# Layer 1's first feed-forward product as pinned 2x2 block products, and layer 2's modulation rows dealt out over output phases, chain and residual

## The chip, the cores and the metric

The kernel runs on one core of one Trainium2 chip. A core has a matrix engine (TensorE, PE in the profile), a vector engine (DVE), an activation engine (ACT), a general engine (POOL) and a sequencer that issues the transfers (SP). Each takes its own instructions in order. The metric is the device time of one execution in microseconds (us), lower is better.

## The reference, cut to what matters

A backbone of two trunk layers over 640 tokens (128 of context, 512 latent), model width 1024, feed-forward width 2816. Context tokens and latent tokens have different conditioning vectors, so each modulation value exists twice.

```
mod = jax.nn.silu(cond) @ p['w_mod'][l] + p['b_mod'][l]        # 6 * 1024 values, for each of 2 conditions
sh_a, sc_a, g_a, sh_f, sc_f, g_f = jnp.split(mod[:, None, :], 6, axis=-1)
xn = rmsnorm(h, p['norm_mix'][l]) * (1 + sc_a) + sh_a
...                                                            # three mixer branches, among them the delta-rule chain
h = h + g_a * y
xf = rmsnorm(h, p['norm_ffn'][l]) * (1 + sc_f) + sh_f
gu = xf @ p['ffn_w_in'][l]                                     # the first feed-forward product
h = h + g_f * ((jax.nn.silu(gu[..., :D_FF]) * gu[..., D_FF:]) @ p['ffn_w_out'][l])
```

## The kernel before, in words

Activations lie with features on the 128 partitions and 640 tokens on the free axis, in two halves of 320 (c = 0, 1). The code counts layers from 0: layer 1 of this text has l = 0, layer 2 has l = 1.

**Products.** A weight block of four 128x128 tiles comes by a transfer of 256 KB (tile wr). ACT rounds it (wh, L514), and POOL (L518) or DVE (L516) takes the remainder (wl). Each 128x128 by 128x320 product is made of three matmuls, high by high, low by high and high by low (lines L563, and L555 for block products). One "128x320" matmul is the unit of work on PE.

**Feed-forward.** The width of 2816 is 22 tiles f. For each f there are a gate product fg and an up product fu (8 k-tiles x 3 x 2 halves = 48 matmuls each, 96 for the pair). The output product is accumulated in groups of f: after each group, fo{group}_{d} for d = 0 to 7 multiplies the group's tiles into the eight output tiles, and the post-processing (h_update, L756, three DVE instructions) adds it to the residual h. Layer 1 has the two groups (0..10), (11..21), all plain. Layer 2 has three groups (0..7), (8..14), (15..21): its first 3 f are plain, and each of the other 19 pairs is made as a 2x2 block product with 7 instead of 8 block multiplications (class Pair; 7 x 4 x 3 = 84 matmuls instead of 96). The price is sums of weight blocks on DVE (L543), sums of token blocks ahead of it (token_sums), and sums of results. In the block stage strict[0] is set: ACT and DVE instructions that go through o() are held in the order in which the program wrote them on their engine.

**Modulation rows.** Class ModVe makes rows m of 48 (6 parts x 8 tiles). For each row a transfer brings the weights (tile wmt, half a row, 256 KB, when nh = 2; a whole row, 512 KB, when nh = 1), and for each of the two conditions one DVE reduction (L638, followed by a read of its accumulator) multiplies it with the conditioning vector and sums up. cond(h) loads half h of the two conditioning vectors (tile cbb) and applies silu: for each condition a tanh on ACT (L624) and one DVE instruction (L625). The wmt tile has bufs slots; a transfer into a slot waits on SP until the reductions that read it are done. In layer 1 the rows 16 to 35 (nh = 2, bufs 4: 80 reductions) run in the delta-rule chain, rows 36 to 39 in the layer's residual product (wo0 to wo7), rows 40 to 47 and all 48 rows of layer 2 in the posts of layer 1's fu products (nh = 1, bufs 4). Layer 2 itself makes no rows.

**Residual and join.** wo0 to wo7 is the mixer's output projection. The posts of its products update h, square it (ACT), and add the square (nacc, DVE L687). wo7 is done in two halves of tokens; each half's end starts the norm (ACT L691, a PE sum cs, ACT L575 and L577), the scaled activations (us L727 or L708, then xh on ACT and xl on DVE, L732 to L734, in layer 1 of before L713 and L720), and these feed the first feed-forward product. This stretch is called the join.

Where an instruction stands on its engine is set by a scheduler over program order and priorities; transfers are all issued by SP, in order.

Of the kernel before, what the change touches and what calls it, by code (L numbers as in the profile page):

```python
# [18 lines left out]
P = 128  # L19
# [11 lines left out]
GROUPS = (((0, 11), (11, 22)), ((0, 8), (8, 15), (15, 22)))  # L31
NPL = (22, 3)
# [380 lines left out]
def tile_hybrid(ctx: ExitStack, tc, a):  # L413
# [197 lines left out]
    class ModVe:  # L611
# [15 lines left out]
        def steps(self, l, ms):  # L627
# [3 lines left out]
            for h in range(self.nh):  # L631
                if self.nh > 1:
                    self.cond(h)
                for m in ms:
                    wm = self.pool.tile([P, self.w], F32, name="wmt", tag="wmt", bufs=self.bufs)
                    dma(wm, a["wmodt"][l, m][:, h * self.w:(h + 1) * self.w])
                    for i in range(2):
                        ins = ve.tensor_tensor_reduce(self.t, wm, self.c[:, i], 0.5, 0.0, ALU.mult, ALU.add,  # L638
                                                      accum_out=acc[h][:, m - m0, i:i + 1])
                        if OPT["pin"] in (1, 2 + self.nh):  # L640
                            tc.keep_in_program_order(ins)
# [8 lines left out]
    def mod_fix(mod, prm, s, d0=0, n=8):  # L650
# [7 lines left out]
        elif s == 2 or s == 5 and mod is mods[0]:  # L658
            ve.tensor_scalar(mod[:, sl], mod[:, sl], 0.5, None, op0=ALU.mult)
# [899 lines left out]
    class Blocks:  # L1559
# [26 lines left out]
        def snap(self, q, i):  # L1586
            t = self.s[q.name, i] = self.sn.tile([P, HF], F32, name="sn", tag="sn", bufs=4)
            o(se.activation(t, self.ps(q, 0), AF.Copy))
# [50 lines left out]
    for l in range(L):  # L1639
# [39 lines left out]
        gr, npl = GROUPS[l], NPL[l]  # L1679
# [127 lines left out]
    for l in range(L):  # L1807
# [107 lines left out]
        with pool("gt", "right", 2) as gt:  # L1915
# [11 lines left out]
            with pool("zs", "left") as zs:  # L1927
# [6 lines left out]
                with pool("bd", "left") as bd, pool("kp", "left") as kp:  # L1934
# [5 lines left out]
                    mst = ModVe(bd, 4, 2).steps(0, range(16, 16 + OPT["mc"])) if l == 0 else iter(())  # L1940
# [14 lines left out]
                    if l == 0:  # L1955
                        mod_fix(mod, prm, 2)
# [15 lines left out]
        mv = ModVe(mvp, 4, 1) if l + 1 < L else None  # L1972
        nm = Norm()
        resid_posts([f"wo{d}.{l}" for d in range(8)], hs, mod[:, 16:24], nm)
        for d in range(7):
            G.to(f"wo{d}.{l}")
            if l == 0:
                mv.run(0, range(16 + OPT["mc"] + (24 - OPT["mc"]) * min(d, 5) // 5, 16 + OPT["mc"] + (24 - OPT["mc"]) * min(d + 1, 5) // 5))
        if l == 0:
            mod_fix(mod, prm, 3)  # L1980
            mod_fix(mod, prm, 4)
        mark(f"normf{l}")
        gr, npl = GROUPS[l], NPL[l]
# [13 lines left out]
        with ExitStack() as fctx:  # L1997
# [8 lines left out]
            def g_post(f):  # L2006
                def post(ps):
                    th = tmp()
                    if l == 0:
                        se.activation(v3(th), ps, AF.Tanh, scale=0.5)  # L2010
                        ve.scalar_tensor_tensor(v3(th), v3(th), 1.0, ps, op0=ALU.add, op1=ALU.mult)
                    else:
                        se.activation(v3(th), ps, AF.Silu)
# [3 lines left out]
            def u_post(f, j):  # L2017
                def post(ps):
# [3 lines left out]
                    if l + 1 < L:  # L2022
                        if l == 0 and f < 8:
                            mv.run(0, [40 + f])
                            if f == 7:
                                mod_fix(mod, prm, 5)
                        mv.run(l + 1, range(48 * f // NF, 48 * (f + 1) // NF))
                return post

            gl_ = len(gr) - 1  # L2030
            for gi, (f0, f1) in enumerate(gr):
# [3 lines left out]
                if gi < gl_:  # L2035
                    for d in range(8):
                        G.posts[f"fo{gi}_{d}.{l}"] = lambda ps, d=d: h_update(hs, d, ps, mod[:, 40:48])
# [64 lines left out]
```

## Time and profile before

| what | value |
|---|---|
| median of three timed executions | 2867.09 us (2866.7 to 2870.57) |
| profiled execution, own time | 2866.79 us |
| its span, first to last instruction | 2865.0 us |
| mean granted TensorE clock | 0.968 of full speed |
| PE busy | 2681.8 us, 94% |
| DVE / ACT / POOL busy | 59% / 45% / 38% |

PE is the engine that is nearly always busy. The times of stretches are read from windows of this one profiled execution; it lies 0.3 us under the median of the timed ones.

### The profile page before, as it was taken

To read this page: it belongs to the slowest core of one execution; us is meant where nothing else is said; L and a number is where in the kernel's file an instruction comes from. 1 tells how busy PE (TensorE), PEld (TensorE's weight loads), DVE (VectorE), ACT (ScalarE), POOL (GpSimd) and SP (SyncE) were. 2 spreads that over 40 slices of the span, in tenths; PEclk is the share of its full clock that TensorE was granted. 3 is DMA by queue.
4 is the path that set the end of the run, shared out by engine and by line. 5 is a ranking of instruction groups with operands and counts; after the bars stand their busy time and mean duration, and the time that the engine had idled before them with its cause. 6 is when DMAs were issued, how large, how long until landed. Compare 5 with 4: busy or idle time off the path is not lost. (4 is left out here: it accounts for less than half of the span.)

```text
span 2865.0 us, 49715 instructions
## 1 busy us (share of the span) xinstructions
PE 2681.8 (94%) x19216; PEld 2461.6 (86%) x19216; DVE 1699.1 (59%) x3141; ACT 1290.1 (45%) x2431; POOL 1075.7 (38%) x777
## 2 busy tenths in 40 slices
PE   6889999899999999999998899997999998999998
PEld 4788887787878899999988888886877898999997
DVE  4765684647655699268456666757434345637373
ACT  5665655543333522122356646565333336425254
POOL 3543222343425467456544432333433254120203
PEclk9999999999999999999999999998999999999999
DMA  6254433245542355335323444232433331222222
GB/s 207 90 163 142 94 77 100 81 113 175 151 113 86 133 175 181 107 123 159 114 80 106 152 136 95 73 97 76 118 98 84 84 108 52 85 85 78 78 80 79
DMA packets 291836, 317.10 MB, mean 111 GB/s; under 512 B 163696, under 2 KB 174768, under 8 KB 291472
## 3 DMA queue, kind: packets, MB, share of 16 engines
q1 hardware_dynamic: 291600, 313.92, 37.4%
q8 instruction: 152, 2.49, 0.4%
q14 instruction: 84, 0.69, 0.1%
HBM read 266.01 MB, written 47.82 MB: 110 GB/s over the span
## 5 line engine op out<-in xcount | busy, mean ns | idle before, releaser
L518 POOL TENSOR_TENSOR wl<-wr,wh 128x512 fp32r<-128x512 f32 (+1 forms) x500 | 723.3, 1450 | 1407.0 <-ACT wh L514 1287.0
L563 PE MATMUL gm<-xh,wh 128*128 128x320 f32 x2848 | 706.2, 324 | 25.6 <-ACT xh L713 7.0
L563 PE MATMUL gm<-xl,wh 128*128 128x320 f32 x2848 | 692.0, 318 | 10.1 <-DVE xl L720 4.2
L563 PE MATMUL gm<-xh,wl 128*128 128x320 f32 x2848 | 687.3, 317 | 15.0 <-POOL wl L518 15.0
L514 ACT ACTIVATE wh<-wr 128x512 fp32r<-128x512 f32 (+1 forms) x538 | 332.4, 621 | 703.7 <-PE gm L563 441.6
L563 PEld LDWEIGHTS gm<-xh,wh 128*128 128x128 f32 x2848 | 487.3, 193 | 50.9 <-ACT xh L713 9.9
L563 PEld LDWEIGHTS gm<-xl,wh 128*128 128x128 f32 x2848 | 491.8, 192 | 27.0 <-DVE xl L720 9.0
L563 PEld LDWEIGHTS gm<-xh,wl 128*128 128x128 f32 x2848 | 489.5, 192 | 23.9 <-POOL wl L518 17.5
L638 DVE CUSTOM_DVE_ANT_0 ctb<-wmt,cbb 128x1024 f32<-128x1024 f32 (+1 forms) x200 | 298.2, 1491 | 3.4
L756 DVE SCALAR_TENSOR_TENSOR h<-gm,mod,h 128x128 f32<-128x128 f32 x168 | 63.8, 433 | 248.7 <-PE gm L563 248.6
L563 PE MATMUL gm<-ah,wh 128*128 128x320 f32 x704 | 164.2, 310 | 0.4 <-DVE h L756 0.2
L563 PE MATMUL gm<-ah,wl 128*128 128x320 f32 x704 | 163.3, 309 | 0.5 <-POOL wl L518 0.5
L563 PE MATMUL gm<-al,wh 128*128 128x320 f32 x704 | 163.3, 309 | 0.0
L1081 ACT ACTIVATE VN<-ch 64x64 f32<-64x64 f32 x320 | 69.9, 219 | 179.7 <-DVE vs L1078 165.5
L563 PEld LDWEIGHTS gm<-ah,wh 128*128 128x128 f32 x704 | 118.3, 188 | 1.7 <-DVE h L756 1.4
L563 PEld LDWEIGHTS gm<-ah,wl 128*128 128x128 f32 x704 | 118.4, 188 | 0.8 <-POOL wl L518 0.8
L563 PEld LDWEIGHTS gm<-al,wh 128*128 128x128 f32 x704 | 118.5, 188 | 0.2
L563 PE MATMUL gm<-ol,wh 128*128 128x320 f32 x384 | 99.0, 331 | 1.5 <-POOL ol L568 1.5
L563 PE MATMUL gm<-oh,wh 128*128 128x320 f32 x384 | 98.4, 333 | 0.5 <-DVE gth L1756 0.3
L563 PE MATMUL gm<-oh,wl 128*128 128x320 f32 x384 | 96.1, 326 | 0.0
L555 PE MATMUL gm<-xh,wl 128*128 128x320 f32 x304 | 94.0, 309 | 0.0
L555 PE MATMUL gm<-xl,wh 128*128 128x320 f32 x304 | 93.9, 309 | 0.0
(793 smaller groups left out, 4743.8 us busy)
## 6 DMA issues: line engine op xcount, KB each, us to landing
wr<-in_wall_dram SPq DMA_DIRECT2D x394, 256.0 KB, 3.0
wmt<-in_wmodt_dram SPq DMA_DIRECT2D x60, 512.0 KB, 3.7
wr<-in_wfo_dram SPq DMA_DIRECT2D x64, 256.0 KB, 2.7
wr<-in_wbr_dram SPq DMA_DIRECT2D x48, 256.0 KB, 2.7
wmt<-in_wmodt_dram SPq DMA_DIRECT2D x40, 256.0 KB, 3.4
wq<-in_wall_dram SPq DMA_DIRECT2D x38, 256.0 KB, 3.1
wm<-in_wmod_dram SPq DMA_DIRECT2D x16, 512.0 KB, 8.4
wr<-in_wfo_dram SPq DMA_DIRECT2D x32, 192.0 KB, 2.4
```

The lines of the kernel that those rows point to most:

```text
L514: o(se.activation(wh[:, :w], wr[:, :w], AF.Copy))
L518: ge.tensor_tensor(wl[:, :w], wr[:, :w], wh[:, :w], op=ALU.subtract)
L555: o(pe.matmul(ps, w_[:, wsl], x_[k], start=(start and i == 0), stop=(stop and i == 2), skip_group_check=True))
L563: o(pe.matmul(ps[:, c, :HF], w_[:, wsl], x_[kx][:, c * HF:(c + 1) * HF], start=(start and i == 0), stop=(stop and i == 2)))
L638: ins = ve.tensor_tensor_reduce(self.t, wm, self.c[:, i], 0.5, 0.0, ALU.mult, ALU.add, accum_out=acc[h][:, m - m0, i:i + 1])
L756: o(ve.scalar_tensor_tensor(hs[d][:, s:e], ps[:, c, s - c * HF:e - c * HF], g[:, d, i:i + 1], hs[d][:, s:e], op0=ALU.mult, op1=ALU.add))
L1081: se.activation(VN[d * 64:(d + 1) * 64, h, n], ps[h * 64:(h + 1) * 64, 1], AF.Copy)
```

## The change

Both layers now use the groups (0..7), (8..14), (15..21) and 3 plain tiles, so layer 1's other 19 pairs become block products too, in the pinned order, with silu by ACT's Silu. The ModVe in the "mv" pool gets nh = 2 and bufs = 2 in place of nh = 1 and bufs = 4, so each set of rows loads the conditioning twice. The rows are dealt out anew: layer 1's rows 36 to 39 (mv0) and the first steps of 40 to 47 (mv1) in its residual product, the rest of mv1 behind its fu1 and fu2; layer 2's rows 0 to 23 (nxt) in the posts of layer 1's output products, 5 reductions for each d in group 0 and 4 in the later ones; its rows 24 to 39 in layer 2's own chain, and 40 to 47 in layer 2's residual product. Inside the pinned stage the reductions are pinned too.

```diff
-GROUPS = (((0, 11), (11, 22)), ((0, 8), (8, 15), (15, 22)))
-NPL = (22, 3)
+GROUPS = ((0, 8), (8, 15), (15, 22))
+NPL = 3
...
-                        if OPT["pin"] in (1, 2 + self.nh):
+                        if strict[0] or OPT["pin"] in (1, 2 + self.nh):
                             tc.keep_in_program_order(ins)
...
-            t = self.s[q.name, i] = self.sn.tile([P, HF], F32, name="sn", tag="sn", bufs=4)
+            t = self.s[q.name, i] = self.sn.tile([P, HF], F32, name="sn", tag="sn", bufs=3)
...
-                    mst = ModVe(bd, 4, 2).steps(0, range(16, 16 + OPT["mc"])) if l == 0 else iter(())
+                    mst = ModVe(bd, 4, 2).steps(l, range(16, 16 + OPT["mc"]) if l == 0 else range(24, 40))
...
-        mv = ModVe(mvp, 4, 1) if l + 1 < L else None
+        mv = ModVe(mvp, 2, 2)
+
+        def some(gen, n):
+            for _ in range(n):
+                if next(gen, 0) == 0:
+                    break
+
+        mv0 = mv.steps(l, range(16 + OPT["mc"], 40)) if l == 0 else iter(())
+        mv1 = mv.steps(l, range(40, 48))
+        nxt = mv.steps(l + 1, range(24)) if l + 1 < L else iter(())
         nm = Norm()
         resid_posts([f"wo{d}.{l}" for d in range(8)], hs, mod[:, 16:24], nm)
         for d in range(7):
             G.to(f"wo{d}.{l}")
-            if l == 0:
-                mv.run(0, range(16 + OPT["mc"] + (24 - OPT["mc"]) * min(d, 5) // 5, 16 + OPT["mc"] + (24 - OPT["mc"]) * min(d + 1, 5) // 5))
+            if l == 0 and d < 4:
+                some(mv0, 4)
+            else:
+                some(mv1, 5)
+        some(mv0, 1000)
...
+        else:
+            some(mv1, 1000)
+            mod_fix(mod, prm, 5)
...
-                    if l == 0:
-                        se.activation(v3(th), ps, AF.Tanh, scale=0.5)
-                        ve.scalar_tensor_tensor(v3(th), v3(th), 1.0, ps, op0=ALU.add, op1=ALU.mult)
-                    else:
-                        se.activation(v3(th), ps, AF.Silu)
+                    se.activation(v3(th), ps, AF.Silu)
...
-                    if l + 1 < L:
-                        if l == 0 and f < 8:
-                            mv.run(0, [40 + f])
-                            if f == 7:
-                                mod_fix(mod, prm, 5)
-                        mv.run(l + 1, range(48 * f // NF, 48 * (f + 1) // NF))
+                    if l == 0 and f:
+                        some(mv1, 8 if f < npl - 1 else 1000)
+                        if f == npl - 1:
+                            mod_fix(mod, prm, 5)
...
+            def fo_post(gi, d):
+                def post(ps):
+                    h_update(hs, d, ps, mod[:, 40:48])
+                    some(nxt, 4 if gi else 5)
+                return post
...
-                        G.posts[f"fo{gi}_{d}.{l}"] = lambda ps, d=d: h_update(hs, d, ps, mod[:, 40:48])
+                        G.posts[f"fo{gi}_{d}.{l}"] = fo_post(gi, d)
...
+            for d in range(6):
+                n = f"fo{gl_}_{d}.{l}"
+
+                def after(*args, post=G.posts[n]):
+                    post(*args)
+                    some(nxt, 4)
+                G.posts[n] = after
```

The order of instructions shows it at three places.

DVE, where layer 1 goes from group 0's output products into the block products of the next group. h_9516 is the last output tile (d = 7), ctb is the reductions' scrap, mod_103 layer 2's modulation. Before, the kernel has such an edge in layer 2 alone:

```order
L756 SCALAR_TENSOR_TENSOR h_23747<-gm,mod_103,h_23747 128x128
L756 SCALAR_TENSOR_TENSOR h_23747<-gm,mod_103,h_23747 128x192
L756 SCALAR_TENSOR_TENSOR h_23747<-gm,mod_103,h_23747 128x320
L516 TENSOR_TENSOR wl<-ws,wh 128x512 x2
L543 TENSOR_TENSOR ws<-wq 128x512
```

After the change, layer 1's edge reads:

```order
L756 SCALAR_TENSOR_TENSOR h_9516<-gm,mod_102,h_9516 128x320
L638 ISA ctb,mod_103<-wmt,cbb 128x512
L638 ISA mod_103 128x1
L638 ISA ctb,mod_103<-wmt,cbb 128x512
L638 ISA mod_103 128x1
L638 ISA ctb,mod_103<-wmt,cbb 128x512
L638 ISA mod_103 128x1
L638 ISA ctb,mod_103<-wmt,cbb 128x512
L638 ISA mod_103 128x1
L638 ISA ctb,mod_103<-wmt,cbb 128x512
L638 ISA mod_103 128x1
L516 TENSOR_TENSOR wl<-ws,wh 128x512 x2
```

Five reductions now stand between the last update and the two remainders wl of the next weights. At the edge from group 1 to group 2 there are four.

DVE, at the end of layer 1's residual product (h_9515 is d = 6, h_9516 is d = 7). Before:

```order
L687 TENSOR_TENSOR nacc<-nacc,th 128x640
L756 SCALAR_TENSOR_TENSOR h_9516<-gm,mod_102,h_9516 128x128
L756 SCALAR_TENSOR_TENSOR h_9516<-gm,mod_102,h_9516 128x192
L756 SCALAR_TENSOR_TENSOR h_9516<-gm,mod_102,h_9516 128x320
L708 TENSOR_TENSOR th<-us_10025,nacc 128x320
```

After:

```order
L687 TENSOR_TENSOR nacc<-nacc,th 128x640
L638 ISA ctb,mod_102<-wmt,cbb 128x512
L638 ISA mod_102 128x1
L756 SCALAR_TENSOR_TENSOR h_9516<-gm,mod_102,h_9516 128x128
L638 ISA ctb,mod_102<-wmt,cbb 128x512
L638 ISA mod_102 128x1
L756 SCALAR_TENSOR_TENSOR h_9516<-gm,mod_102,h_9516 128x192
L638 ISA ctb,mod_102<-wmt,cbb 128x512
L638 ISA mod_102 128x1
L638 ISA ctb,mod_102<-wmt,cbb 128x512
L638 ISA mod_102 128x1
L756 SCALAR_TENSOR_TENSOR h_9516<-gm,mod_102,h_9516 128x320
```

Between the conditioning's two L625 behind d = 4 and this last update stand 16 reductions. In layer 2's residual product, which had none, 16 stand ahead of d = 3's update, then the conditioning, and 16 more ahead of d = 6's.

ACT, in layer 1's second group of output products, where the second half of nxt's conditioning comes in; each pair of wh (128x512 and 128x384) is the weight of one d. Before, this place held only such weights:

```order
L514 ACTIVATE wh<-wr 128x512 x2
L514 ACTIVATE wh<-wr 128x384
L514 ACTIVATE wh<-wr 128x512 x2
```

After:

```order
L514 ACTIVATE wh<-wr 128x384
L514 ACTIVATE wh<-wr 128x512
L624 ACTIVATE ctb<-cbb 128x512 x2
L514 ACTIVATE wh<-wr 128x384
L514 ACTIVATE wh<-wr 128x512
```

Two tanh of the conditioning now stand ahead of the weight of d = 3's second half.

## Rows read from the trace of the kernel before

**Rows 1.** The page: busiest engine; two costliest weight preparations (busy, mean ns).

```profile
PE 2681.8 (94%) x19216; PEld 2461.6 (86%) x19216; DVE 1699.1 (59%) x3141; ACT 1290.1 (45%) x2431; POOL 1075.7 (38%) x777
...
L518 POOL TENSOR_TENSOR wl<-wr,wh 128x512 fp32r<-128x512 f32 (+1 forms) x500 | 723.3, 1450 | 1407.0 <-ACT wh L514 1287.0
...
L514 ACT ACTIVATE wh<-wr 128x512 fp32r<-128x512 f32 (+1 forms) x538 | 332.4, 621 | 703.7 <-PE gm L563 441.6
```

**Rows 2.** What PE waited for, 1000 to 1460 us, layer 1's feed-forward.

```profile
PE gm L563 <- POOL wl L518: 0.6, 1, 0.6
```

**Rows 3.** Windows: us, PE, PEld, DVE, ACT, POOL busy (count), PEclk, DMA share, GB/s.

```profile
1050.00:1100.00 50.00, 50.00 (x343) 50.00 (x342) 49.15 (x55) 11.33 (x19) 33.81 (x18) 1.00 0.57 181
2450.00:2500.00 50.00, 50.00 (x343) 50.00 (x342) 35.11 (x57) 24.73 (x44) 3.07 (x3) 1.00 0.25 79
```

**Rows 4.** Groups of DVE by form: busy us, mean ns, idle before.

```profile
L638 DVE CUSTOM_DVE_ANT_0 ctb<-wmt,cbb 128x512 f32<-128x512 f32 x80 | 68.7, 859 | 0.3
...
L638 DVE DVE_READ_ACCUMULATOR2_ANT mod<- 128x1 f32 x160 | 12.4, 78 | 0.0
```

**Rows 5.** Transfers: count, KB each, median us from issue to landing.

```profile
wmt<-in_wmodt_dram SPq DMA_DIRECT2D x40, 256.0 KB, 3.4
...
cbb<-in_condb_dram SPq DMA_DIRECT2D x2, 512.0 KB, 5.0
```

**Rows 6.** Line L638: shortest/median/longest ns, first and last start.

```profile
L638 DVE CUSTOM_DVE_ANT_0 ctb<-wmt,cbb x200: 673/1224/2480, 652.1 to 1390.3; 128x1024 f32<-128x1024 f32 x60, 128x512 f32<-128x512 f32 x40
```

**Rows 7.** Line L624, the conditioning's tanh on ACT, likewise.

```profile
L624 ACT ACTIVATE ctb<-cbb x6: 629/632/1064, 647.2 to 926.6; 128x512 f32<-128x512 f32 x4, 128x1024 f32<-128x1024 f32 x2
```

**Rows 8.** Line L625, the conditioning's DVE instruction, likewise.

```profile
L625 DVE SCALAR_TENSOR_TENSOR cbb<-ctb,cbb x6: 681/694/1227, 649.7 to 927.7; 128x512 f32<-128x512 f32 x4, 128x1024 f32<-128x1024 f32 x2
```

**Rows 9.** Timeline (start, us) of layer 2's edge from group 0 to block products.

```profile
2580.34 1.13 DVE L756 SCALAR_TENSOR_TENSOR h<-gm,mod,h 128x128 f32<-128x128 f32 x3 [5.31 <-PE gm L563]
...
2581.39 1.28 DVE L516 TENSOR_TENSOR wl<-ws,wh 128x512 fp32r<-128x512 f32 x2
...
2582.04 0.31 PE L555 MATMUL gm<-xl,wh 128*128 128x320 f32 x1
...
2582.19 0.35 PE L555 MATMUL gm<-xh,wl 128*128 128x320 f32 x1
```

**Rows 10.** Windows at and behind a PE stall of 4.83 us, in layer 2's first part.

```profile
1545.50:1551.00 5.50, 0.67 (x5) 0.41 (x3) 5.45 (x5) 1.78 (x4) 5.50 (x5) 0.74 0.30 116
1551.00:1555.00 4.00, 4.00 (x15) 4.00 (x16) 3.60 (x3) 0.30 (x1) 2.79 (x2) 0.51 0.68 211
```

**Rows 11.** Windows of 80 us around the joins of layers 1 and 2, alike in phase.

```profile
946.96:1026.96 80.00, 73.69 (x449) 69.30 (x448) 55.64 (x89) 39.79 (x74) 38.42 (x27) 0.94 0.34 110
2369.16:2449.16 80.00, 71.08 (x425) 66.46 (x424) 44.43 (x81) 47.96 (x86) 35.45 (x25) 0.91 0.19 59
```

**Rows 12.** Timeline of DVE at the end of layer 1's residual product.

```profile
954.26 1.13 DVE L756 SCALAR_TENSOR_TENSOR h<-gm,mod,h 128x128 f32<-128x128 f32 x3 [0.66 <-PE gm L563]
...
956.20 0.83 DVE L687 TENSOR_TENSOR nacc<-nacc,th 128x640 f32<-128x640 f32 x1 [0.81 <-ACT th L686]
...
976.96 0.55 DVE L756 SCALAR_TENSOR_TENSOR h<-gm,mod,h 128x320 f32<-128x320 f32 x1 [4.42 <-PE gm L563]
```

**Rows 13.** The same for layer 2's residual product.

```profile
2369.43 1.14 DVE L756 SCALAR_TENSOR_TENSOR h<-gm,mod,h 128x128 f32<-128x128 f32 x3 [4.27 <-PE gm L563]
...
2390.55 1.13 DVE L756 SCALAR_TENSOR_TENSOR h<-gm,mod,h 128x128 f32<-128x128 f32 x3 [4.28 <-PE gm L563]
...
2394.07 0.68 DVE L756 SCALAR_TENSOR_TENSOR h<-gm,mod,h 128x128 f32<-128x128 f32 x2 [0.75 <-PE gm L563]
2399.16 0.55 DVE L756 SCALAR_TENSOR_TENSOR h<-gm,mod,h 128x320 f32<-128x320 f32 x1 [4.42 <-PE gm L563]
```

**Rows 14.** Windows over the chains of layers 1 and 2, to the same place.

```profile
641.00:917.50 276.50, 269.48 (x2238) 222.24 (x2237) 174.91 (x490) 95.42 (x252) 103.59 (x78) 0.98 0.44 127
2071.00:2341.07 270.07, 263.80 (x2238) 219.41 (x2237) 109.86 (x322) 93.48 (x249) 99.78 (x79) 0.99 0.32 86
```

More of the change, by code (lines that the diff above doesn't have):

```diff
@@ L657, in mod_fix @@
                                     op0=ALU.add, op1=ALU.mult)
-        elif s == 2 or s == 5 and mod is mods[0]:
+        elif s == 2:
             ve.tensor_scalar(mod[:, sl], mod[:, sl], 0.5, None, op0=ALU.mult)
@@ L1678, in tile_hybrid @@
             k8(f"wo{d}", "post" if d == 7 else None)
-        gr, npl = GROUPS[l], NPL[l]
+        gr, npl = GROUPS, NPL
         pairs = {f: Pair(f"ff{f}.{l}", a["wall"][l, TILES[f"fg{f}"]], a["wall"][l, TILES[f"fu{f}"]]) for f in range(npl, NF)}
@@ L1954, in tile_hybrid @@
                         pass
-                    if l == 0:
-                        mod_fix(mod, prm, 2)
+                    for s_ in (2,) if l == 0 else (3, 4):
+                        mod_fix(mod, prm, s_)
                     G.to(f"br1_7.{l}")
@@ L1981, in tile_hybrid @@
             mod_fix(mod, prm, 4)
+        else:
+            some(mv1, 1000)
+            mod_fix(mod, prm, 5)
         mark(f"normf{l}")
-        gr, npl = GROUPS[l], NPL[l]
+        gr, npl = GROUPS, NPL
         if npl < NF:
@@ L2008, in post @@
                     th = tmp()
-                    if l == 0:
-                        se.activation(v3(th), ps, AF.Tanh, scale=0.5)
-                        ve.scalar_tensor_tensor(v3(th), v3(th), 1.0, ps, op0=ALU.add, op1=ALU.mult)
-                    else:
-                        se.activation(v3(th), ps, AF.Silu)
+                    se.activation(v3(th), ps, AF.Silu)
                     st[f] = th
@@ L2049, in tile_hybrid @@
             if l + 1 < L:
-                for s_ in range(6):
+                some(nxt, 1000)
+                for s_ in range(3):
                     mod_fix(mods[l + 1], prms[l + 1], s_)
```

## The prediction

> **What bounds the kernel now.** The page first: PE is busy 94% of the span, the next engine DVE 59% [rows 1]. A share is a mean over stages, so next the waits of PE in the stretch that the change rewrites, layer 1's feed-forward from 1000 to 1460 us: all there is comes to 0.6 us [rows 2]. Then windows inside it: 343 matmuls in 50 us with PE busy for all 50, at full clock, though DVE is busy for 49.15 of them with modulation rows [rows 3]. Layer 2's block stage, at 2450 us, runs at the same 343 in 50 us with DVE at 35.11 [rows 3]. So both kinds of feed-forward are bound by the number of matmuls, 50 / 343 = 0.1458 us each, and DVE's load there costs nothing today. What is gained is matmuls; what can be lost is a place where PE must wait for the work that is dealt out anew. One quantity decides most of these: the modulation rows take DVE time and a transfer each, and they move from where DVE's queue was harmless (behind plain products) to where PE waits for the very next DVE instruction.
>
> **Matmuls saved.** 19 pairs x 12 = 228 matmuls of 128x320 go, nothing is added on PE but what follows. 228 x 0.1458 = **-33.2 us**. Both rates of [rows 3] are equal, so this term holds as long as PE is fed.
>
> **The edges from output products to block products.** Layer 2 has this edge in before: the last update of h runs from 2580.34 for 1.13 us, right behind it the two remainders wl from 2581.39 for 1.28 us, so the first is ready about 2582.03, and PE uses it at 2582.19 [rows 9]. The slack is 0.16 us. In layer 1 after the change, five reductions (then four, at the second edge) stand in that gap, in pinned order. A reduction of 512 takes 0.859 us on average and the read of its accumulator 0.078 [rows 4], 0.94 together; the shortest of any is 0.673 [rows 6]. Five and four of them less the slack: 5 x 0.94 - 0.16 = 4.5 and 4 x 0.94 - 0.16 = 3.6, **+8.1 us**. From below, at 0.75 each: 3.6 + 2.8 = 6.4. From above: five steps are two and a half weight tiles, and there are two slots now, so the third tile may have to land (3.4 us [rows 5]) behind the first one's reductions, up to 3 us more: 11.1. The other six posts of a group hide theirs, since their h is not the last and the next product's weights are POOL's work.
>
> The Trainium skill, page "GPSIMD Engine Reference", section "Specifications", says that GpSimd shares its SBUF interfaces with VectorE and contends with DVE instructions that have two SBUF inputs, as a reduction has. Around an edge POOL is nearly idle (3.07 of 50 us in [rows 3]), so by that rule the edge's reductions would be short ones, and the term 6.4 instead of 8.1, the whole sum 1.7 lower. I keep the mean, since the rows don't tell short from long by what POOL did.
>
> **The conditioning's second half in group 1.** nxt has 24 rows x 2 = 48 reductions per half: 40 in group 0's eight posts, 8 in the posts of d = 0 and 1 of group 1. The next half of the conditioning goes into the same tile, so its transfer waits for reduction 48. A product of group 1 is 7 x 3 x 2 = 42 matmuls, 6.1 us. d = 1 ends 12.3 us into the group; h 1.13 and four reductions 3.75 make 17.1; the transfer lands 5.0 later [rows 5], 22.1; tanh 0.63 [rows 7], the DVE instruction 0.69 [rows 8], tanh again, 24.1. Only then does ACT do the weight of d = 3's second half, 0.62, and POOL its remainder, 1.45 [rows 1]: 26.1. PE is there at three products and four tiles, 18.4 + 3.5 = 21.9 us. So up to 4.0 us of PE; none if reduction 48 was early or the weight stands ahead in time. I take **+3.5** (0 to 4).
>
> **The clock behind these stalls.** Where PE is busy for only 0.67 of 5.50 us, a stall of 4.83, the clock falls: the window 1551 to 1555 behind it has PE busy for 4.00 us, a granted clock of 0.51, the lower of the two levels (1.2 GHz), and only 15 matmuls, where 27.4 would go at 343 in 50 us [rows 10]. The 12.4 that are missing are 1.8 us. My three stalls (4.5, 3.5, 3.6) are shorter than the 4.83 seen, so I count half for each, **+2.7** (0 to 5.4).
>
> The Trainium skill, page "TensorE: Matmul & The Clock Gate", section "What's actually happening", says that the throttled 1.2 GHz is the engine's default and that activity releases it, at 2.4 GHz; rows 10 show a fall and a release of that kind. By that rule read strictly, each of the three would pay in full, 5.4 us, 2.7 more in the whole sum.
>
> **First block products of layer 1.** Two more tiles' conditioning and some rows stand between their wl on DVE. DVE had 14.9 idle us in 50 in this kind of stage [rows 3]; five reductions are 4.7. **+1** (0 to 3, a row transfer's landing).
>
> **Token sums at layer 1's join.** They exist in layer 2's join only. Windows of 80 us that begin 30 us ahead of the last update of h in each layer hold 449 matmuls in layer 1 and 425 in layer 2 [rows 11]: 24 x 0.1458 = **+3.5** (2 to 4; the sums are the difference that I know of).
>
> **Layer 1's residual product.** One product is 48 matmuls, 7.0 us. The last conditioning of mv1 starts after the 16th reduction, ahead of d = 4's update at 954.26 [rows 12]; landed 5.0, twice 0.63 + 0.69 = 2.6: about 961. Then 16 reductions, 8 tiles, stand ahead of the last update. With two slots, a slot's next tile lands 3.4 us after its reductions end, while the other tile's two take 1.9, so a tile goes by in (3.4 + 1.9) / 2 = 2.6 us: 2 x 1.9 + 6 x 2.6 = 19.6, end at 980.6. Three updates of 1.13 and two nacc adds of 0.83 stand between, 5 us, in part within the waits. The last update was at 976.96 [rows 12], so it comes 3.6 to 8.6 late, and what follows it is the join that PE waits for. **+6** (0, if rows land much sooner, to 9).
>
> **Layer 2's residual product.** The same with 16 reductions ahead of d = 3's update, at 2369.43 now, and 16 ahead of d = 6's, at 2390.55 [rows 13]. Conditioning after the first 16: 2369 to 2371 + 5.0 + 2.6 = 2377 to 2379, then 19.6: 2396.5 to 2398.5; d = 6's update, a nacc add, 2.0: d = 7's first half at 2398.5 to 2400.5 for 2394.07, 4.4 to 6.4 late; a share of two updates and two adds on top. The second half, at 2399.16, has 5 us of cover, but the norm of the first half has none. **+7** (0 to 9).
>
> **Layer 2's chain with 64 reductions.** Layer 1's chain, with 80, takes 276.5 us for 2238 matmuls, layer 2's, without, 270.07 for the same 2238 [rows 14]. 6.4 x 64 / 80 = 5.1 is the most; the clock's 0.98 beside 0.99 is part of it. **+4** (0 to 5.1).
>
> Silu in place of tanh and one DVE instruction, three slots for snapshots, and fewer reductions in layer 1's feed-forward cost nothing and give nothing: PE was full there.
>
> **The sum.** 8.1 + 3.5 + 2.7 + 1 + 3.5 + 6 + 7 + 4 = 35.8, less 33.2: +2.6 on the profiled execution's 2866.8 (span 2865.0 and 1.8 around it; 0.3 under the median): **2869.4 us**. What a measurement of this kernel can tell from no change is about 0.2%, 5.7 us: the forecast is no change, chance 0.36. The gain is there and is given back in small stalls.
>
> **Rivals.**
> - The residuals hide their rows. The deciding number is the time per row tile: layer 1 has 16 us for 8 tiles, so at 2.0 us or less (landing in about 2 us, or three landings in flight) nothing comes late. For it: SP often issues early. Against it: 3.4 us to landing, two slots. Then those two and the chain cost 1 each: 35.8 - 14 = 21.8, **2855 us**, chance 0.22. That the edges and group 1 hide too, all lower ends: 8.4 of cost, **2842**, chance 0.11.
> - Slower: DVE becomes the bound of both residual products, not only of their ends. Per product five steps are 2.5 tiles of 2.6 us, 6.6, and an update and an add 2.0: 8.6 for a product of 7.0. If results are so released late that PE waits for a bank, 1.5 us for each of four products is lost in either residual on top of the join: +12, **2881 us**, chance 0.20. It decides at the same 2.0 us per tile, from above, if PE's banks run out before the join. Against it: in before DVE was busy 49 of 50 us and PE waited for nothing, but there with four slots.
> - The edges at their upper ends, with the third tile late and the clock paid in full (11.1 + 4 + 5.4 for 14.3): **2876 us**, chance 0.11.
>
> So faster by over 0.2% 0.33, within 0.36, slower 0.31. The range that leaves out no more than 2 in 10 goes from 2846, inside the all-hidden case, to 2884, over the second rival; the forecast's own range is 2861 to 2873.
>
> **What the changed profile would show.** Matmuls 228 fewer, and 343 in 50 us in layer 1's block stage. At layer 1's two edges a PE idle of 4.5 and 3.6 us that ends with DVE's wl L516, with reductions ahead of it; in group 1, 22 us in, an idle that ends with POOL's wl after L624. The clock under 1 behind them. In the residuals, row tiles 2.6 us apart, and the last update of h 3.6 to 8.6 us later against PE's last matmul than now. Layer 2's chain some 4 us longer. The prediction is wrong if the edges show no idle (rows done in the shade), if the joins start as early as now, or if PE waits in a place that I name nowhere, transfers on SP behind a wait for a row slot above all.

## The result, and the profile after

The changed kernel takes 2914.48 us (median of 4 runs, 2913.95 to 2917.34) where the kernel before took 2868.61: the ratio is 1.0162, 95% interval 1.0144 to 1.018. It is 1.6% slower; the forecast was no change, and the time lies 30 us over the range. The profiled execution has a span of 2912.3 us, 47.3 more than before's.

The page of the changed kernel, the rows that answer to [rows 1] and [rows 4]:

```profile
PE 2689.2 (92%) x18988; PEld 2457.5 (84%) x18988; DVE 1854.9 (64%) x3711; ACT 1379.1 (47%) x2605; POOL 902.0 (31%) x682
...
L638 DVE CUSTOM_DVE_ANT_0 ctb<-wmt,cbb 128x512 f32<-128x512 f32 x320 | 287.7, 899 | 28.8 <-DMA wmt<-in_wmodt_dram 24.6
```

The 228 matmuls are gone (19216 less 18988), so the 33.2 us were saved, and 80.5 us were lost elsewhere. DVE now waits 24.6 us for row tiles before reductions; no such wait stood in [rows 4]. Where PE's time went is read from windows cut at the stages' borders. The changed kernel, in order: layer 1's residual product, fg0 to fu2, block group 0, output group 0, block group 1, output group 1, block group 2, output group 2 with the join into layer 2, all of layer 2 up to its residual product, and that product:

```profile
921.60:997.20 75.60, 62.40 (x376) 57.96 (x374) 52.36 (x108) 30.38 (x54) 27.85 (x20) 0.93 0.60 195
997.20:1055.90 58.70, 49.58 (x288) 47.97 (x289) 52.12 (x96) 34.48 (x63) 23.20 (x16) 0.85 0.24 75
1055.90:1126.20 70.30, 66.38 (x446) 65.02 (x445) 57.05 (x101) 34.38 (x63) 3.77 (x2) 1.00 0.31 96
1126.20:1182.60 56.40, 56.40 (x387) 56.40 (x386) 33.72 (x86) 12.06 (x20) 20.20 (x15) 1.00 0.53 155
1182.60:1276.30 93.70, 89.02 (x590) 88.76 (x590) 70.87 (x127) 45.65 (x82) 1.80 (x1) 0.96 0.27 82
1276.30:1329.80 53.50, 51.16 (x338) 50.49 (x336) 37.80 (x84) 11.77 (x22) 18.73 (x15) 0.97 0.52 157
1329.80:1413.30 83.50, 80.91 (x543) 80.65 (x542) 64.15 (x115) 42.12 (x75) 1.30 (x1) 0.98 0.25 77
1413.30:1482.05 68.75, 58.74 (x369) 55.74 (x369) 42.55 (x93) 30.94 (x56) 27.51 (x22) 0.95 0.44 142
1482.05:2341.70 859.65, 795.77 (x5910) 696.43 (x5911) 536.32 (x1111) 428.35 (x848) 297.20 (x226) 0.95 0.38 108
2373.80:2451.30 77.50, 63.72 (x377) 59.86 (x375) 53.28 (x104) 29.87 (x52) 28.98 (x21) 0.89 0.51 170
```

The kernel before, the stretches that answer to the first, the second, the eighth, the ninth and the tenth:

```profile
920.20:981.70 61.50, 57.31 (x376) 54.84 (x375) 32.27 (x54) 29.72 (x51) 28.93 (x19) 1.00 0.59 201
981.70:1034.80 53.10, 50.19 (x300) 47.74 (x301) 45.49 (x66) 21.05 (x40) 28.67 (x19) 0.91 0.33 102
1378.90:1461.30 82.40, 80.31 (x538) 78.63 (x536) 28.33 (x47) 32.17 (x56) 37.17 (x30) 1.00 0.36 106
1461.30:2310.65 849.35, 783.70 (x5906) 688.05 (x5906) 482.72 (x975) 426.12 (x844) 295.74 (x226) 0.95 0.36 98
2343.10:2403.90 60.80, 57.41 (x380) 55.46 (x379) 17.48 (x34) 28.06 (x48) 25.64 (x21) 1.00 0.39 130
```

A stretch less its matmuls at 0.1458 us is what PE lost in it. Output group 0 lost nothing with five reductions behind each product (56.4 for 387), block group 1 lost 93.7 - 86.0 = 7.7. The two residual products stand out: the same 376 matmuls take 75.6 us instead of 61.5, and 77.5 instead of 60.8 (377 and 380 matmuls). PE's idle grew there by 9.0 and 10.4 us, and its busy time, for the same work, by 5.1 and 6.3, at a granted clock of 0.93 and 0.89 where it was 1.00.

Who waits for whom has turned round there. What DVE waited for in layer 2's residual product, before (2343.1 to 2403.9):

```profile
DVE h L756 <- PE gm L563: 27.1, 8, 4.4
```

and in the changed kernel (2373.8 to 2451.3):

```profile
DVE cbb L625 <- ACT ctb L624: 8.5, 4, 4.4
DVE h L756 <- PE gm L563: 6.8, 1, 6.8
DVE ctb L638 <- DMA wmt<-in_wmodt_dram: 4.4, 4, 2.5
```

Before, DVE stood ready for each of the eight products. Now it does so once, for the second half of the last one; every earlier result was done while h's update still stood behind other work, mostly reductions, the conditioning or a row tile. Three updates of h in DVE's timeline in this stretch of the changed kernel:

```profile
2398.90 1.13 DVE L756 SCALAR_TENSOR_TENSOR h<-gm,mod,h 128x128 f32<-128x128 f32 x3
...
2404.23 1.66 DVE L638 CUSTOM_DVE_ANT_0 ctb<-wmt,cbb 128x512 f32<-128x512 f32 x1
2405.93 0.69 DVE L638 CUSTOM_DVE_ANT_0 ctb<-wmt,cbb 128x512 f32<-128x512 f32 x1
...
2407.28 1.13 DVE L756 SCALAR_TENSOR_TENSOR h<-gm,mod,h 128x128 f32<-128x128 f32 x3
...
2418.24 0.35 DVE L756 SCALAR_TENSOR_TENSOR h<-gm,mod,h 128x128 f32<-128x128 f32 x1
```

These updates come 8.4 and 11.0 us apart, not 7.04 as in [rows 13] (2369.43 to 2390.55 are three products). The lateness goes on to PE through ACT; its timeline in the same stretch, and then PE's, show how:

```profile
2407.66 0.40 ACT L702 ACTIVATE us<-h,mod 128x128 f32<-128x128 f32 x1 [5.21 <-DVE h L756]
...
2412.10 0.63 ACT L624 ACTIVATE ctb<-cbb 128x512 f32<-128x512 f32 x1 [2.30 <-DMA cbb<-in_condb_dram]
2412.64 0.61 ACT L514 ACTIVATE wh<-wr 128x512 fp32r<-128x512 f32 x1
```

```profile
2413.30 0.56 PE L563 MATMUL gm<-xh,wh 128*128 128x320 f32 x2 [2.20 <-ACT wh L514]
```

ACT stands at the prescale of h (L702) for 5.2 us, then at the conditioning's transfer for 2.3 more, and the next weight's wh, which uses the result of neither, goes only behind them. PE is idle for 2.20 us until it has that wh.

At the edge into block group 1 the picture is the forecast's. DVE in the changed kernel, and then PE in the same stretch:

```profile
1187.36 0.69 DVE L638 CUSTOM_DVE_ANT_0 ctb<-wmt,cbb 128x512 f32<-128x512 f32 x1 [1.39 <-DMA wmt<-in_wmodt_dram]
...
1188.71 1.29 DVE L516 TENSOR_TENSOR wl<-ws,wh 128x512 fp32r<-128x512 f32 x2
```

```profile
1189.45 0.64 PE L555 MATMUL gm<-xh,wl 128*128 128x320 f32 x1 [4.68 <-DVE wl L516]
1189.89 0.47 PE L555 MATMUL gm<-xh,wh 128*128 128x320 f32 x1
1190.15 0.47 PE L555 MATMUL gm<-xl,wh 128*128 128x320 f32 x1
```

Five reductions, among them a wait of 1.39 us for the third tile, then wl, and 4.68 us of idle PE; behind it matmuls start 0.26 us apart: the granted clock is 0.50 from 1189.45 to 1193, the lower of the two levels.

### The profile page after: what moved, and what is told of

Same layout as the page of the kernel before. It is cut to its first block, busy times and chain, and to the rows that moved or that the text cites. A ratio compares the mean times of both kernels' runs of the same rounds, so it can differ in the third digit from the quotient of the medians.

```text
span 2912.3 us, 50151 instructions
## 1 busy us (share of the span) xinstructions
PE 2689.2 (92%) x18988; PEld 2457.5 (84%) x18988; DVE 1854.9 (64%) x3711; ACT 1379.1 (47%) x2605; POOL 902.0 (31%) x682
## 4 chain that ended last, share of the span: by engine, by line
PE 45%; DVE 10%; issue 4%; ACT 4%; DMA 3%; POOL 2%; SPq 1%; DVEq 0%; POOLq 0%; ACTq 0%
PE gm L563 23%; PE gm L555 16%; PE ch L1041 2%; DVE ctb L638 1%; POOL wl L518 1%; PE psc L1266 1%; DVE S L1497 1%; DMA wmt<-in_wmodt_dram 1%; POOL xl L1761 1%; PE pmo L1298 1%; DVE R L976 1%; DVE xl L734 1%; SPq L429 1%; PE ppt L1281 1%; DMA cbb<-in_condb_dram 1%
## 5 line engine op out<-in xcount | busy, mean ns | idle before, releaser
L518 POOL TENSOR_TENSOR wl<-wr,wh 128x512 fp32r<-128x512 f32 (+1 forms) x424 | 596.3, 1411 | 1629.5 <-ACT wh L514 1425.5
L563 PE MATMUL gm<-xh,wh 128*128 128x320 f32 x2240 | 572.8, 331 | 33.2 <-ACT wh L514 10.2
L514 ACT ACTIVATE wh<-wr 128x512 fp32r<-128x512 f32 x500 | 305.9, 619 | 436.8 <-PE gm L563 232.9
L563 PEld LDWEIGHTS gm<-xh,wh 128*128 128x128 f32 x2240 | 392.8, 197 | 57.2 <-ACT wh L514 11.5
L563 PEld LDWEIGHTS gm<-xh,wl 128*128 128x128 f32 x2240 | 394.3, 196 | 32.4 <-POOL wl L518 23.7
L563 PEld LDWEIGHTS gm<-xl,wh 128*128 128x128 f32 x2240 | 396.2, 196 | 29.7 <-DVE xl L734 9.2
L638 DVE CUSTOM_DVE_ANT_0 ctb<-wmt,cbb 128x512 f32<-128x512 f32 x320 | 287.7, 899 | 28.8 <-DMA wmt<-in_wmodt_dram 24.6
L514 ACT ACTIVATE wh<-ws 128x512 fp32r<-128x512 f32 x152 | 95.7, 630 | 128.2 <-PE gm L555 72.8
L555 PE MATMUL gm<-xeh,wh 128*128 128x320 f32 x456 | 141.3, 310 | 2.6 <-ACT sn L1588 2.6
L555 PE MATMUL gm<-xeh,wl 128*128 128x320 f32 x456 | 141.3, 310 | 0.9 <-DVE wl L516 0.9
L555 PE MATMUL gm<-xel,wh 128*128 128x320 f32 x456 | 141.6, 311 | 0.0
```

The source lines that it names most:

```text
L514: o(se.activation(wh[:, :w], wr[:, :w], AF.Copy))
L518: ge.tensor_tensor(wl[:, :w], wr[:, :w], wh[:, :w], op=ALU.subtract)
L555: o(pe.matmul(ps, w_[:, wsl], x_[k], start=(start and i == 0), stop=(stop and i == 2), skip_group_check=True))
L563: o(pe.matmul(ps[:, c, :HF], w_[:, wsl], x_[kx][:, c * HF:(c + 1) * HF], start=(start and i == 0), stop=(stop and i == 2)))
```

## The experiments

Two theories were set against each other first. **PLACE**: row work costs where PE's next work stands behind it in an engine's order, and nearly nothing where it does not. **TRANSFERS**: what costs are the row and conditioning transfers with two slots, wherever they stand. And a third, **BLOCKS**: layer 1's block products lose what they save.

**x1_no_rows**, all rows outside the chains left out:

```diff
-        mv0 = mv.steps(l, range(16 + OPT["mc"], 40)) if l == 0 else iter(())
-        mv1 = mv.steps(l, range(40, 48))
-        nxt = mv.steps(l + 1, range(24)) if l + 1 < L else iter(())
+        mv0, mv1, nxt = iter(()), iter(()), iter(())
```

> All rows outside the two chains are left out (layer 1's rows 36 to 47, layer 2's 0 to 23 and 40 to 47: no transfers, no conditioning, no reductions, zeros in their place). Theory PLACE (the loss is row work standing ahead of work that PE waits for): of the 80 us that were lost against the 33 saved, only token sums (some 6), layer 2's chain (7) and its first part (2) stay, so 2914.5 - 65 = about 2850 us (2845 to 2857). Theory BLOCKS (layer 1's block products themselves cost more than they save): above 2885 us, with PE idle inside layer 1's block stage and its edges as in the changed kernel.

Measured: 2852.84 us (ratio to before 0.9949, 0.9935 to 0.9964), 62 us less than the changed kernel. BLOCKS has fallen. Layer 1's residual product is back:

```profile
917.80:977.90 60.10, 56.74 (x375) 54.80 (x373) 17.40 (x35) 28.01 (x48) 25.60 (x21) 1.00 0.39 132
```

**x2_short_rows**, reductions of 32 columns instead of 512:

```diff
+                        n_ = self.w if self.bufs == 4 else 32
-                        ins = ve.tensor_tensor_reduce(self.t, wm, self.c[:, i], 0.5, ...
+                        ins = ve.tensor_tensor_reduce(self.t[:, :n_], wm[:, :n_], self.c[:, i, :n_], 0.5, ...
```

> All transfers, slots, conditioning loads and the number of reductions outside the chains stay, but each of these reductions reads only 32 of its 512 columns (the rest of the sum is left out). Theory PLACE by DVE time: 120 of the 160 rows' halves cost little, and what stays is the conditioning and the landing of the rows: 2862 to 2880 us. Theory TRANSFERS (row and conditioning transfers with two slots hold SP, and weights behind them come late): above 2895 us, with the same ACT wh waits on transfers in both residual products.

Measured: 2890.96 us (2883.7 to 2898.3), between the two: the shorter reductions are worth 23.5 us of the 62, and 38 stay. The profiled execution is the slowest of the four, 2898.32. In layer 2's residual product DVE is busy for 35.6 us, not 53.3 (17.5 without rows, as x4 shows), and its updates are still late. The stretch, and DVE's timeline in it:

```profile
2362.90:2435.25 72.35, 61.73 (x377) 57.01 (x375) 35.60 (x104) 29.23 (x52) 26.39 (x21) 0.94 0.54 181
...
2377.11 0.19 DVE L639 CUSTOM_DVE_ANT_0 ctb<-wmt,cbb 128x32 f32<-128x32 f32 x1 [4.76 <-DMA wmt<-in_wmodt_dram]
...
2377.47 1.13 DVE L757 SCALAR_TENSOR_TENSOR h<-gm,mod,h 128x128 f32<-128x128 f32 x3
```

An update of h, whose product is done, stands behind an instruction of 0.19 us that waits 4.76 us for its tile, and at 2397.53 another stands behind the conditioning, for which DVE waited 5.45 us.

**x3_clear_edges**, none behind the last output product of groups 0 and 1:

```diff
-                    some(nxt, 4 if gi else 5)
+                    some(nxt, 0 if d == 7 else 5 if gi else 6)
```

> Same rows, but none behind the last output product of group 0 and of group 1: six reductions behind d = 0 to 6 in group 0, five in group 1 (five and four before). Theory PLACE: PE's idle of 4.7 and 2.6 us at the two edges and the slow matmuls behind them go, 8.1 + 4.9 us lost there become 1.5: 11 us less, 2903 us (2900 to 2906). Theory TRANSFERS: the same number of rows over the same stretch, 2910 us or more.

Measured: 2910.87 us, 3.6 less, not 11: by the time alone it lies in TRANSFERS' range. But the edges did go; the windows of block group 1, output group 1 and block group 2:

```profile
1185.70:1273.50 87.80, 86.37 (x590) 86.11 (x590) 69.24 (x122) 45.62 (x82) 1.80 (x1) 1.00 0.26 84
1273.50:1331.30 57.80, 52.11 (x338) 51.70 (x338) 39.90 (x96) 12.02 (x22) 18.42 (x15) 0.94 0.50 156
1331.20:1411.60 80.40, 79.42 (x542) 79.16 (x542) 62.69 (x110) 42.12 (x75) 1.30 (x1) 1.00 0.23 76
```

What PE waited for in output group 1 (1273 to 1332):

```profile
PE gm L563 <- ACT wh L514: 5.7, 1, 5.7
```

5.9 and 3.1 us were gained in the block groups, and output group 1 gave 4.3 back: with reductions dealt out otherwise, the conditioning came one product earlier in ACT's order, and PE's idle behind it grew from 2.3 to 5.7 us. Output group 0, with six reductions behind each of seven products, took the same 56.4 us. The rest, 3.1 us, lies ahead of group 0, where the change of the program does not reach.

**x4_wo2_to_chain**, layer 2's rows 40 to 47 into its chain:

```diff
-                    ... if l == 0 else range(24, 40))
+                    ... if l == 0 else range(24, 48))
-        mv1 = mv.steps(l, range(40, 48))
+        mv1 = mv.steps(l, range(40, 48)) if l == 0 else iter(())
```

> Layer 2's rows 40 to 47 (32 reductions, two conditioning loads less) go from its residual product into its chain, which then makes 96 reductions instead of 64. Theory PLACE: the residual product and its join get back to before's (17 us less), the chain pays 32/64 of the 7 us it lost: 2914.5 - 17 + 3.5 = 2901 us (2897 to 2905). If rows cost the same wherever they stand: 2912 us or more.

Measured: 2906.91 us, 7.6 less: between the two ranges, nearer to PLACE. Layer 2 up to its residual product, and that product:

```profile
1480.34:2351.13 870.79, 796.18 (x5931) 697.94 (x5932) 559.71 (x1176) 428.71 (x849) 302.61 (x227) 0.95 0.39 112
2381.80:2442.00 60.20, 56.81 (x376) 54.86 (x375) 17.49 (x35) 28.08 (x48) 25.73 (x21) 0.99 0.39 132
```

The residual product is back at 60.2 us, all 17 us, but the chain is no free place: 64 reductions cost the stretch 859.65 - 849.35 = 10.3 us less four matmuls, 9.7; 96 cost it 17.8.

The next three ask which ingredient of a row makes the residual products slow. **COND** says the waits for the conditioning, **ROWS** the row transfers.

**x5_cond_first**, the conditioning loaded once:

```diff
-            if nh == 1:
+            if nh == 1 or bufs == 2:
                 self.cond(0)
...
-                if self.nh > 1:
+                if self.nh > 1 and self.bufs != 2:
                     self.cond(h)
```

> The conditioning is loaded once when the rows outside the chain begin and not loaded again for the other halves (the sums then use the wrong half's values); all rows, transfers and reductions stay. Of the 62 us between the changed kernel and the one without rows, 38 stayed when the reductions were cut to 32 columns. Theory COND (the waits for the conditioning's transfer in ACT's and DVE's order are most of these 38): 2885 to 2895 us. Theory ROWS (the row transfers with two slots are): 2905 us or more.

**x6_no_row_loads**, two row tiles read over and over:

```diff
-                    wm = self.pool.tile([P, self.w], F32, name="wmt", tag="wmt", bufs=self.bufs)
-                    dma(wm, a["wmodt"][l, m][:, h * self.w:(h + 1) * self.w])
+                    if self.bufs != 2 or len(self.kept) < 2:
+                        ...
+                        self.kept.append(wm)
+                    else:
+                        wm = self.kept[self.n % 2]
```

> All reductions and all conditioning loads stay, but only the first two row tiles are loaded outside the chains; the later reductions read these two again (wrong sums, no transfer, no wait for a slot on SP). Theory ROWS: reductions run back to back and SP is never held by them, 2875 to 2895 us. Theory COND: 2902 us or more.

**x7_silu_stored**, the finished silu written to memory once and loaded from there:

```diff
         def cond(self, h):
+            if h in stored:
+                dma(self.c, SCND[h])
+                return
```

> The changed kernel, but the silu of the conditioning is written to memory once in layer 1's chain, and every later load brings the finished values: no tanh on ACT and no DVE instruction with it. Theory COND by ACT (ACT's in-order wait for the conditioning holds up weights and squares): about half of COND's share back, 2890 to 2905 us. Theory ROWS, or COND by the landing alone: 2909 us or more.

Measured: 2895.75 (2886.3 to 2900.3), 2900.33 (2896.4 to 2901.4) and 2904.14 us (2896.0 to 2911.4): 19, 14 and 10 us less than the changed kernel. The kernel before took 2865.21 beside them, 3.4 less than beside the changed kernel, so some 3 us of each difference may not be theirs. x5 lies just over COND's range, x6 between both, x7 at the upper end of the range for waits on ACT: neither COND nor ROWS is the cause alone. Layer 2's residual product, without the conditioning's second load (first, an execution of 2886.33 us) and without row transfers (second, 2899.41):

```profile
2351.40:2423.20 71.80, 61.80 (x379) 57.92 (x377) 52.87 (x103) 28.56 (x50) 29.16 (x21) 0.92 0.55 176
```

```profile
2367.00:2437.00 70.00, 60.51 (x379) 56.44 (x377) 50.76 (x105) 29.69 (x52) 28.51 (x21) 0.98 0.41 136
```

With all of it the product takes 77.5 us, without rows 60.2; with short reductions 72.35, without a second load of the conditioning 71.8, without row transfers 70.0. Each ingredient taken away gives back 5 to 7.5 of 17: what is left still holds up h's update. Together they come to 18.4 for 17.3, nearly a plain sum.

**x8_rows_in_blocks**: the stored silu, the next half fetched with the last reduction of the half before, rows pinned, none in the residual products but layer 1's rows 36 to 39, and rows in the block stage instead (the first lines below; more() gives one reduction of mv1 or nxt).

```diff
+                        if m == ms[-1] and i == 1:
+                            nh_ = h + 1 if h + 1 < self.nh else then
+                            if nh_ is not None:
+                                self.cond(nh_)
...
         def mul(self, q):
             ...
+            self.more()      # also at the end of c12, c22 and low
...
-                    if l == 0 and f:
-                        some(mv1, 8 if f < npl - 1 else 1000)
+                    if f < 2:
+                        some(mv1, 8)
...
+                    if gi == 0 and d < 7:
+                        some(nxt, 7 if d < 6 else 6)
```

> The stored silu, each next half of it loaded as soon as the last reduction of the half before is issued, rows held in program order, and the rows dealt so that nothing that PE waits for stands behind them: in the residual products only layer 1's rows 36 to 39 behind d = 0 to 3; rows 40 to 47 of both layers behind fu0 and fu1 (8 reductions each) and one for every fourth instruction group in the first block group; layer 2's first 24 rows behind d = 0 to 6 of group 0 (48 reductions) and one at a time in the later block groups; none behind the output products of groups 1 and 2. Theory PLACE: all but the token sums (6), layer 2's chain (7), its first part (2) and a few us in the first block group go: 2855 to 2866 us, a little faster than the kernel before (2867). If rows cost about 0.3 us each wherever they stand once PE is not plain: above 2885 us.

Measured: 2870.77 us, ratio to before 1.0021 (1.0008 to 1.0034): 44 us less than the changed kernel, and 5 over the upper end of what was hoped. In the profiled execution, of 2875.57 us, output group 0 and block group 1 lose 3.4 and 8.2 us:

```profile
1103.80:1163.50 59.70, 56.78 (x386) 56.32 (x385) 43.34 (x109) 12.03 (x20) 21.38 (x15) 1.00 0.56 172
1163.50:1257.90 94.40, 87.87 (x591) 87.60 (x589) 87.39 (x182) 45.00 (x82) 1.79 (x1) 0.96 0.39 123
```

Seven reductions for each 7 us product are more than row tiles keep up with: in output group 0 DVE waited 12 times for one, 10.8 us in all. The backlog came out at the edge, where PE waited 6.5 us for wl.

**x9_rows_spread** deals them thinner:

```diff
-                    if gi == 0 and d < 7:
-                        some(nxt, 7 if d < 6 else 6)
+                    if gi == 0 and d < 6:
+                        give(5)
+                    if gi == 1 and d < 7:
+                        give(4)
...
+                elif f0now[0] == 2 or f0now[1] < 48:
+                    give(1)
```

> The kernel with rows in the block stage, where 48 reductions behind seven output products of group 0 were too many: PE lost 3.9 us in group 0 and 8.8 in the block group behind it, 6.5 of them at the edge. Now five behind d = 0 to 5, 18 one at a time in the second block group, four behind d = 0 to 6 of group 1, 20 in the third block group; the conditioning's second half is fetched as soon as reduction 48 is issued. Theory PLACE: both groups lose 0.5 to 1 us, so 2870.8 - 11 = 2860 us (2856 to 2864), faster than the kernel before by about 0.2%. If what was lost there was the number of rows: 2868 us or more.

Measured: 2858.61 us, ratio to before 0.9981 (0.9964 to 0.9999), with every row made: 0.2% under the kernel before, by an interval that ends just short of 1, and in the range of PLACE. It differs from the changed kernel in several things at once (stored silu, early fetch, pinned order, dealing); what each gives was not taken apart. Layer 1's residual product with its 16 reductions, block group 0, block group 1, then block group 2, and layer 2's residual product:

```profile
922.00:982.90 60.90, 57.19 (x376) 54.89 (x374) 34.54 (x69) 26.95 (x48) 27.48 (x21) 1.00 0.59 198
...
1038.20:1103.70 65.50, 65.50 (x447) 65.12 (x446) 62.14 (x121) 33.11 (x60) 3.77 (x2) 1.00 0.39 130
...
1160.00:1246.20 86.20, 86.20 (x590) 86.17 (x589) 77.63 (x153) 45.38 (x82) 1.80 (x1) 1.00 0.35 113
...
1295.40:1374.60 79.20, 79.20 (x542) 79.16 (x542) 73.20 (x153) 41.70 (x75) 1.92 (x2) 1.00 0.32 102
...
2332.30:2392.80 60.50, 57.10 (x379) 55.16 (x377) 18.43 (x34) 27.98 (x48) 25.62 (x21) 1.00 0.44 146
```

DVE is busy for 77.6 of 86.2 us in block group 1, with 18 reductions in pinned order between the remainders wl, and PE is never idle. And layer 1's residual product takes 16 reductions, with their row transfers but without the conditioning's tanh, for 0.7 us (60.9, and 60.1 in x1 without any for one matmul less): such a product is not dear for any number of rows.

**x10_blocks_alone**, no rows in layer 2's chain either:

```diff
-                    mst = ModVe(bd, 4, 2).steps(l, range(16, 16 + OPT["mc"]) if l == 0 else range(24, 40))
+                    mst = ModVe(bd, 4, 2).steps(l, range(16, 16 + OPT["mc"])) if l == 0 else iter(())
```

> The kernel without rows outside the chains, with layer 2's rows 24 to 39 in its chain left out too: block products in layer 1 and nothing else of the change. From the sum: 2867 - 33.2 + 3.5 to 6 (token sums) = 2837 to 2840 us if 64 reductions cost the chain 7 us or more and layer 2's first part 2; 2846 us if the chain's share is what the stretches of the changed kernel showed and the first part is not touched. 2852 us or more if the chain's reductions are free and the block products lose elsewhere.

Measured: 2839.95 us (ratio 0.9903, 0.9887 to 0.992), 26.3 under before, and 12.9 under x1_no_rows (13.2 by the two ratios): the share of the chain's rows. Its fg0 to fu2, and output group 2 with the join:

```profile
982.10:1036.90 54.80, 48.60 (x288) 46.56 (x289) 36.22 (x63) 33.55 (x62) 23.91 (x15) 0.89 0.17 54
1373.30:1435.80 62.50, 56.80 (x370) 54.08 (x368) 21.21 (x39) 31.28 (x56) 25.08 (x21) 0.99 0.36 112
```

So the block products alone bring 26.3 of the 33.2. The join into layer 2 loses 62.5 - 370 x 0.1458 = 8.6 us here and 82.4 - 538 x 0.1458 = 4.0 before. A reason that was only argued: the last product has 7 tiles f now, not 11, so the half under which the norm of the other half hides is 21 matmuls, 3.1 us, instead of 33, 4.8.

## Why the prediction was wrong

| step | put | measured, and from what |
|---|---|---|
| matmuls | -33.2 | 228 fewer; -26.3 net without rows (x10) |
| ahead of layer 1's residual | 0 | +1.4 (921.6 for 920.2) |
| layer 1's residual | +6 | +14.1 (75.6 for 61.5) |
| token sums | +3.5 | +3.4 (fg0 to fu2 in x10: 54.8 us for 288 matmuls, 12.8 lost; before 53.1 for 300, 9.4 lost), and +3.9 more there with rows (58.7 for 54.8) |
| first block products | +1 | +5.0 (5.3 lost; x9 0.3) |
| two edges, with their clock | +9.9 | +11.6 (7.7 and 4.3 lost, less 0.4) |
| conditioning in group 1, with its clock | +4.4 | +4.2 |
| join into layer 2 | 0 | +10.9 (14.9 lost for 4.0), 4.6 of it without rows |
| layer 2's chain | +4 | +9.7 (all of layer 2 up to its residual) |
| layer 2's residual | +7 | +16.7 (77.5 for 60.8) |

The costs in the right column come to 80.9; less 33.2 that is 47.7, and the span says 47.3.

Right were the saving, the token sums, the place and releaser of both edges, the stall in group 1 (the conditioning landed, two tanh, then wh, PE idle for 2.17 us), and that output products hide five reductions each. That the edges and group 1 came out within 2 us of what was put, 15.8 for 14.3, is in part luck: PE's idle was 9.6 us where 11.6 were put, and the matmuls behind cost 6.6 us more than at full clock where 2.7 were put. At the first edge, too, two errors met: the reductions took 0.68 or 0.69 us, not 0.859, and a wait of 1.39 us for a tile made up for it.

Of what the two pages of the Trainium skill added, the clock's fall behind each stall was borne out, in the strict reading that the sum did not take: 3.0, 1.7 and 1.9 us behind idles of 4.7, 2.6 and 2.3 us, where it put half of 1.8. The Trainium skill, page "TensorE: Matmul & The Clock Gate", section "What's actually happening", has the engine throttled by default; the trace agrees, with matmuls 0.26 us apart instead of 0.1458 behind the 4.68 us. (Rows 10 show the fall alone; the release lies behind them, from 1555 to 1560 us, at a granted clock of 1.00.) The shared interface showed at the edge, where POOL was idle and all reductions were short ones, and at another place, where it was not (last section). One slip is without weight: 2 x 1.9 + 6 x 2.6 is 19.4 us, not 19.6.

Wrong was the step on the two residual products, "+6" and "+7", which measured 14.1 and 16.7 us. It asked how late the last update would be, with rows at 2.6 us a tile, and let the product itself run at 7.0 us. But every update stands in the same queue. When it is late, ACT's prescale and square are late, the next weight's wh stands behind them, PE stalls within the product, and the product comes later still. The second rival named DVE as the bound of each product, and the deciding figure, but it had PE wait for banks, where PE waited for ACT's wh (4.8 us in layer 2's product), and it priced four products at 1.5 us on top of the join; of the six gaps between the updates of d = 0 to 6, five were 8.4 to 11.0 us in layer 2's product and four 9.0 to 12.3 in layer 1's. The sum also put at nothing the clock behind these stalls: 5.1 and 6.3 us of the loss are PE's longer busy time.

That rows in this place cost the 17 us x4 shows (without them, 60.2 us); that it is not one cost, x2, x5 and x6, which each leave 70 us or more. That the delays add up in one queue is read from the timelines above and fits the near sum of 18.4. A ring is part of it, as far as the waits go: the row tile that DVE waits for is issued by SP in order with weights, and those wait for slots that POOL and ACT free, which wait for DVE. This ring was not cut by itself, so its own share stays open, and so does the number of rows at which a residual product begins to pay: 16 without tanh cost 0.7 us in x9, 32 with the conditioning's loads and tanh 17 us.

Two smaller steps failed the same way. In the first block products, "+1", the conditioning's tanh stood ahead of ACT's snapshot sn: ACT waited 6.4 us for its transfer, and PE's longest idle of the stretch ended with that snapshot, not with a wl.

```profile
PE gm L555 <- ACT sn L1588: 2.6, 1, 2.6
```

And the sum does not hold the join into layer 2 at all: rows behind d = 0 to 5 of the last group delay the squares of its norm, and the last product is shorter (x10). The chain's "+4" took the difference of two stretches as an upper bound for 80 reductions; 64 cost 9.7 us and, in x1 against x10, 12.9. The two stretches were of two different layers, so their difference was no bound.

## What to carry to other kernels

Work that is dealt out to "idle" time of an in-order engine costs little where nothing urgent is queued behind it; ahead of an instruction that another engine's queue waits for, it costs its waits too (a transfer, a conditioning, a slot), once for each product, and the chain of queues passes them on. So ask of each place what stands next in that queue, not how idle the engine is: the pinned block stage of x9, with DVE at 90 to 92%, took 18 to 20 reductions a group for nothing, one at a time, while layer 2's residual product, with DVE at 29% before, took 32 for 17 us. And a price taken from two different stages is no bound: price it by taking the work away.

## What the runs showed of the hardware

A reduction of 512 took 0.69 us at most places and 1.5 to 1.8 us at others, at the same shape. In layer 2's residual product ten of the 32 were long, and all ten began while POOL was at work on a remainder; none of the other 22 did. At 2404.23 us (1.66, quoted above) POOL had two remainders in hand, and at 2405.93, when these were done, the next took 0.69. The rows of POOL there, in the changed kernel:

```profile
2402.01 3.33 POOL L518 TENSOR_TENSOR wl<-wr,wh 128x512 fp32r<-128x512 f32 x2 [5.78 <-ACT wh L514]
```

It is not a slower rate. In x2_short_rows a reduction of 32 columns, 0.19 us elsewhere, took 1.17 beside a remainder on POOL and ended 0.05 us after it:

```profile
2369.26 1.28 POOL L518 TENSOR_TENSOR wl<-wr,wh 128x512 fp32r<-128x512 f32 x1 [2.68 <-ACT wh L514]
2369.42 1.17 DVE L639 CUSTOM_DVE_ANT_0 ctb<-wmt,cbb 128x32 f32<-128x32 f32 x1
```

The Trainium skill, page "GPSIMD Engine Reference", section "Specifications", says that GpSimd shares its SBUF interfaces with VectorE and contends with DVE instructions that have two SBUF inputs. The trace agrees, with 1.66 for 0.69 us at 512 columns, a factor of 2.4, and 1.17 for 0.19 at 32. It is a part of why rows are dearer in a residual product, where POOL prepares the weights, than in the block stage, where POOL was busy for 1.8 of 86.2 us. It is not the whole: output group 0 hid its reductions with POOL busy for 20.2 of 56.4 us.
